# A two-layer decoder step in split float32: another order of the down projection's chunks, of the norm's products and of the last additions, and of the places of the recurrence

## The chip, the cores and the metric

The kernel runs on one core of a Trainium2 chip. The metric is the time of one execution on the device in microseconds; the runs of a kernel are given by their median.

## The reference

One inference step of a decoder with two layers, an mLSTM layer and a forgetting-attention (FoX) layer, each followed by a SwiGLU FFN. A prompt of 1024 tokens behind 16 meta tokens and 8 requests of 8 tokens each go through the same weights: 1104 tokens of 1024 values, d_ff = 2816.

```python
for l in range(DEPTH):
    if l < N_A_LAYERS:
        a, (C, n, m) = mlstm_mixer(rmsnorm(h, norm_a), C0, n0, m0, lead, w_in_a, ...)
        h = h + a                          # out = (rmsnorm(heads) * sigmoid(og)) @ w_out
    else:
        h = h + fox_mixer(rmsnorm(h, norm_b), shared, attend, w_qo_b, q_norm_b, w_out_b)
    h = h + swiglu(rmsnorm(h, norm_ffn[l]), w_gate_up[l], w_down[l])
    if l == N_A_LAYERS - 1:
        shared = shared_kv(h, norm_kv, w_kvf, b_fg_b, k_norm_b)
y = rmsnorm(h, norm_final)

def swiglu(xn, w_gu, w_d):
    gu = xn @ w_gu
    return (silu(gu[..., :D_FF]) * gu[..., D_FF:]) @ w_d
```

It returns y for both groups, the recurrent states of both, and the new keys, values and log-forget values.

## The kernel before

The activations stand transposed: 128 partitions hold features, columns are tokens. The 1104 tokens are three groups (`TS`: 336, 384 and 384 columns, t = 0, 1, 2). Every float32 operand of a product is split into a high part and a low part (L243 the cast on ScalarE, `h`; L244 the subtraction on VectorE, `l`), and each product is three matmuls: high by high, high by low, low by high (L170 to 172, L1589). A norm needs the sum over the features of the squares: `add_sq` squares each of 8 tiles on ScalarE (`nq`, two buffers) and adds it to `ns` on GpSimd, the last one on VectorE; one matmul with ones (`nps`) adds over the partitions; ScalarE takes the root into `nr`, VectorE the reciprocal.

The FFN of a layer ends with the down projection in `ffn`. Its first group takes two rounds of 11 steps; groups 1 and 2 are computed together in seven rounds of a fast 2 x 2 block product (`rounds`: B11, T2, B21, T3, T4, T1, B22), z = 0 to 6. The 11 chunks of a round are taken as `groups`: a single chunk, then five pairs. A step of a pair has 24 matmuls into four PSUM banks (`dps`, of six), a single chunk 12. Rounds z = 1, 4 and 6 go on adding in the banks of the round before. At the last step of a round the banks are added to the residual (L1255; `goes` says to which halves: 12 additions after z = 1, 4 after the others). Each step also starts the split of weights two steps on (`w_split`), of activations (`h_split`), a load of activations on GpSimd's queue (`h_load`) and one of weights five steps on, on SyncE's (`w_load`). During these rounds the program order on TensorE, VectorE and ScalarE is the order in which the code is written.

Between the matmuls of these rounds run the next norm's steps: `norm_x` is a generator, and `ends(t)` makes it the current one of `steps`, from which each step of the down projection takes one piece, two at z > 4:

```python
for _ in range(2 if t and z > 4 else 1):
    next(steps, None)
```

In layer 0 the next norm is that of keys, values and the attention; for groups 0 and 1 it writes its product (L334, VectorE) to a PSUM tile `npy`, copies it to `xh` (L335, ScalarE) and subtracts that for `xl` (L337, VectorE). The group 2 norm comes after the last round; the value products (`tmps`, `first_values`) of the other groups fill in there, from weights that `early` has loaded and split (`first_weights`, the 256 value columns of w_kvf, L237 and L238; other columns, 272 wide, follow). In layer 1 the next norm is the final one (`final`: `fss` one matmul per tile, L1635 to 1657 the root, `fin` transposes, L1670 the product with root and gain).

In layer 0 `mlp` also multiplies the output gates into the heads (L1217): `heads` loads gate tiles `ogc` on GpSimd's queue (L665) into a place of three buffers with the tag `ny`. The pool of these tiles takes the space that the recurrence's tiles held before. There the state C is updated, read by TensorE (L1121), and in the end written out as out_p_C and out_p_n (L927, L928); `gates`, `tmA`, `den`, `ssqA` and the later `rd` and `fA` (L1189 to 1200, the heads' norm) stand beside it. When a new tile takes a place, its first writer waits for what used the place before. Names in the traces carry the tile's name: `vA` and `Ht` are the residual in layer 0 and 1, `slot`, `fs` and `ws` weights, `hr` raw activations.

## Time and profile before

| | us |
|---|---|
| runs, median (lowest to highest) | 2932.83 (2931.76 to 2937.74) |
| profiled execution, its time | 2933.44 |
| profiled execution, its span | 2931.7 |
| TensorE busy in it | 2831.8 (97%) |
| VectorE busy | 1686.1 (58%) |
| ScalarE busy | 1150.9 (39%) |
| GpSimd busy | 826.8 (28%) |

A busy share is over the whole span; a stretch with its own limit shows only in the rows of that stretch. In these, "x" counts instructions, and the granted clock is that of TensorE, 1.00 being full. In a timeline's row the first number is the start, the second the busy time, and in brackets stands the idle time before it and what ended it.

### The profile page before, as it was taken

Reading aid. Unit: us, or ns where it says so; the run is one execution under the profiler, and the core shown is the slowest. Engines: PE = TensorE matmul, PEld = TensorE weight load, DVE = VectorE, ACT = ScalarE, POOL = GpSimd, SP = SyncE. Lnnn points to the kernel's source line nnn. Section 1 sums busy time; section 2 is a strip of 40 time slices with the busy share of each in tenths; the row PEclk is TensorE's granted clock in tenths of the full one; section 3 lists DMA queues with packets and bytes.
Section 4 is the critical chain, followed back from the end, with each engine's and each line's share of the span. In section 5 each row is a group of like instructions: output and inputs, shape, how many; then the busy total and the mean of one; then the engine's idle time right before and its main releaser. Section 6 shows DMA issues by size and latency. Waiting matters only on the chain.

```text
span 2931.7 us, 53400 instructions
## 1 busy us (share of the span) xinstructions
PE 2831.8 (97%) x20709; PEld 2708.8 (92%) x20709; DVE 1686.1 (58%) x3292; ACT 1150.9 (39%) x2103; POOL 826.8 (28%) x1228
## 2 busy tenths in 40 slices
PE   7999999999999999989999999999999999999998
PEld 7989888999999999989999887777899999999998
DVE  5032565876676555763354442677467676665565
ACT  5222363322222244443344453777432222224343
POOL 2011232332232221224353201454232322322122
PEclk9999999999999999999999999999999999999999
DMA  7153545244444375645453685443324454436574
GB/s 249 48 129 94 146 151 151 96 136 154 155 145 151 114 250 189 223 159 159 138 166 127 218 297 202 144 151 128 120 78 143 143 166 145 142 117 225 190 249 151
DMA packets 382631, 464.43 MB, mean 158 GB/s; under 512 B 38594, under 2 KB 303770, under 8 KB 381354
## 3 DMA queue, kind: packets, MB, share of 16 engines
q1 hardware_dynamic: 341058, 323.68, 34.7%
q0 software_dynamic: 37648, 135.03, 14.1%
q8 instruction: 163, 2.67, 0.4%
q10 hardware_dynamic: 3672, 2.31, 0.3%
q14 instruction: 90, 0.74, 0.1%
HBM read 324.63 MB, written 136.29 MB: 157 GB/s over the span
## 4 chain that ended last, share of the span: by engine, by line
PE 77%; DVE 6%; ACT 3%; issue 2%; DMA 2%; POOL 1%; DVEq 0%; SPq 0%; POOLq 0%; ACTq 0%
PE m L1274 22%; PE dps L1589 15%; PE fps L172 4%; PE fps L171 4%; PE fps L170 4%; PE tmps L171 3%; PE tmps L170 3%; PE tmps L172 3%; PE pops L172 2%; PE pops L171 2%; PE pops L170 2%; PE sp L2341 1%; PE op L2428 1%; DVE s L2345 1%; PE bps L170 1%
## 5 line engine op out<-in xcount | busy, mean ns | idle before, releaser
L244 DVE TENSOR_TENSOR slot<-slot,slot 128x1024 fp32r<-128x1024 f32 (+1 forms) x152 | 191.8, 1264 | 119.6 <-ACT slot L243 119.3
L243 ACT CAST slot<-slot 128x1024 fp32r<-128x1024 f32 (+1 forms) x152 | 152.8, 1007 | 184.6 <-PE dps L1589 78.7
L172 PE MATMUL fps<-x0h,slot 128*128 128x336 f32 x688 | 218.2, 317 | 1.6 <-DVE slot L244 1.6
L170 PE MATMUL fps<-x0h,slot 128*128 128x336 f32 x688 | 218.3, 317 | 0.0
L171 PE MATMUL fps<-x0l,slot 128*128 128x336 f32 x688 | 217.4, 316 | 0.0
L1274 PE MATMUL m<-x2h,slot 128*128 128x384 f32 x704 | 193.7, 336 | 0.0
L1274 PE MATMUL m<-x1h,slot 128*128 128x384 f32 x672 | 184.7, 336 | 0.0
L172 PEld LDWEIGHTS fps<-x0h,slot 128*128 128x128 f32 x688 | 129.1, 188 | 2.1 <-DVE slot L244 2.1
L170 PEld LDWEIGHTS fps<-x0h,slot 128*128 128x128 f32 x688 | 129.3, 188 | 0.6 <-ACT slot L243 0.3
L171 PEld LDWEIGHTS fps<-x0l,slot 128*128 128x128 f32 x688 | 129.5, 188 | 0.3
L1274 PEld LDWEIGHTS m<-x2h,slot 128*128 128x128 f32 x704 | 128.5, 188 | 0.0
L1274 PEld LDWEIGHTS m<-x1h,slot 128*128 128x128 f32 x672 | 122.5, 188 | 0.0
L1589 PE MATMUL dps<-T_1h,slot 128*128 128x384 f32 x448 | 119.2, 340 | 2.4 <-ACT T_1h L243 2.4
L1274 PE MATMUL m<-x2l,slot 128*128 128x384 f32 x352 | 118.5, 337 | 0.0
L1589 PE MATMUL dps<-T_2h,slot 128*128 128x384 f32 x448 | 118.5, 340 | 0.0
L244 DVE TENSOR_TENSOR slot<-Ht,slot 128x1024 fp32r<-128x1024 f32 x59 | 83.7, 1419 | 54.5 <-ACT slot L243 54.5
L244 DVE TENSOR_TENSOR slot<-vA,slot 128x1024 fp32r<-128x1024 f32 x59 | 83.6, 1418 | 54.6 <-ACT slot L243 54.6
L1274 PE MATMUL m<-x1l,slot 128*128 128x384 f32 x336 | 112.8, 336 | 0.0
L316 POOL TENSOR_TENSOR ns<-ns,nq 128x384 f32<-128x384 f32 (+1 forms) x68 | 76.6, 1126 | 126.3 <-ACT nq L314 124.0
L1274 PE MATMUL m<-T_2h,slot 128*128 128x384 f32 x352 | 97.7, 338 | 2.0 <-DVE slot L244 2.0
L2368 ACT ACTIVATE s<-s,nb 128x272 f32<-128x272 f32 (+7 forms) x126 | 98.9, 787 | 0.0
L1274 PE MATMUL m<-T_4h,slot 128*128 128x384 f32 x352 | 97.8, 338 | 0.0
(775 smaller groups left out, 9176.8 us busy)
## 6 DMA issues: line engine op xcount, KB each, us to landing
slot<-in_w_down SPq DMA_DIRECT2D x48, 512.0 KB, 4.3
slot<-in_w_gate_up SPq DMA_DIRECT2D x36, 512.0 KB, 4.2
ws<-in_w_down SPq DMA_DIRECT2D x88, 192.0 KB, 3.0
sD<-ws SPq DMA_DIRECT2D x88, 192.0 KB, 2.2
kp<-in_cache_k SPq DMA_DIRECT2D x32, 512.0 KB, 6.0
vp<-in_cache_v SPq DMA_DIRECT2D x32, 512.0 KB, 5.3
hr<-hB_T POOLq DMA_DIRECT2D x40, 384.0 KB, 5.2
vA<-in_w_gate_up SPq DMA_DIRECT2D x26, 512.0 KB, 3.9
```

What stands on the lines that cost most here:

```text
L170: mm(ps, sh, mh, start=first, stop=False)
L171: mm(ps, sh, ml, start=False, stop=False)
L172: mm(ps, sl, mh, start=False, stop=last)
L243: self.nc.scalar.copy(hi, src)
L244: self.nc.vector.tensor_tensor(out=lo, in0=src, in1=hi.bitcast(F32), op=ALU.subtract)
L316: (nc.vector if x >= late else nc.gpsimd).tensor_tensor(out=s, in0=s, in1=sq, op=ALU.add)
L1274: nc.tensor.matmul(u.ps[b], w[p][:, k], x[q][:, k], start=first and k == i == 0, stop=k == 3 and i == 2, skip_group_check=True)
L1589: nc.tensor.matmul(o, p[:, k, ms], q[:, k], start=fresh and k == x == 0, stop=last and k == nk - 1 and x == 2, skip_group_check=True)
L2341: nc.tensor.matmul(ps[z][:, :n], a[r, qs], b[r, at : at + n], start=(y == 0), stop=(y == 2))
L2345: nc.vector.tensor_tensor_reduce(out=ss[z, u][:, at + o : at + e], in0=ps[z][:, o:e], in1=diag[x][:, z] if y else ncb[:, z, at + o : at + ...
L2368: nc.scalar.activation(ss[z, u], ss[z, u], AF.Exp, bias=nb[:, z : z + 1], accum_out=sm[:, u, z : z + 1])
L2428: mm(po[ds[z], :256], vr[:, j0 + x, ds[z]], th[:, x, z], start=(j0 + x == 0), stop=False)
```

## The change

- `groups` puts the single chunk at the end of each round, behind five pairs.
- `norm_x` for groups 0 and 1 of layer 0 makes products 0 and 1 ahead; each later piece copies one product, subtracts its low, and makes the product two ahead. For group 2 the next pair of products is made ahead of the low.
- Two pieces of a norm per step only at odd steps of z > 4, none at the last step of z = 1, else one.
- At the last step of the down projection the four additions come ahead of all squares; for group 2 the last four sums of squares are added on VectorE.
- `first_weights` loads its raw tiles at two earlier steps (into a weight slot and `fs0`) and splits them at the steps where it had loaded and split them before.
- The state C is given its place ahead of `gates` in the pool of layer 0's recurrence, and in the pool of the FFN the first `ns`, `nq`, `nr` and the third gate tile are given theirs first.

```diff
             if then and i % 3 == 2:
                 then(i // 3)
 
+    def place(self, sp, nm, bufs):
+        if nm in self.first:
+            return self.first.pop(nm)
+        return sp.tile([P, SL], F32, name=self.uid(nm), tag=nm, bufs=bufs)
+
     def add_sq(self, H, t, m, sp, x, late=KT - 1):
 
         nc = self.nc
...
         if x == 0:
-            self.sums[t] = sp.tile([P, SL], F32, name=self.uid("ns"), tag="ns", bufs=2)
+            self.sums[t] = self.place(sp, "ns", 2)
             nc.scalar.activation(self.sums[t][:, :n], H[t][:, m], AF.Square)
             return
-        sq = sp.tile([P, SL], F32, name=self.uid("nq"), tag="nq", bufs=2)[:, :n]
+        sq = self.place(sp, "nq", 2)[:, :n]
         nc.scalar.activation(sq, H[t][:, m], AF.Square)
         s = self.sums[t][:, :n]
         (nc.vector if x >= late else nc.gpsimd).tensor_tensor(out=s, in0=s, in1=sq, op=ALU.add)
...
         xh, xl = self.new_x(t)
-        for k in range(KT if psum else 0):
-            y = pp.tile([P, 512], F32, name=self.uid("npy"), tag="n")[:, :n]
-            nc.vector.tensor_tensor(out=y, in0=H[t][:, k], in1=r, op=ALU.mult)
-            nc.scalar.copy(xh[:, k], y)
-            yield
-            nc.vector.tensor_tensor(out=xl[:, k], in0=y, in1=xh[:, k].bitcast(F32), op=ALU.subtract)
-        for z in range(0 if psum else 4):
-            ks = slice(2 * z, 2 * z + 2)
-            y = H[t][:, ks] if inplace else self.ny(self.uid("ny"))[:, :, :n]
+        if psum:
+
+            ys = {}
+
+            def product(k):
+                if k < KT:
+                    ys[k] = pp.tile([P, 512], F32, name=self.uid("npy"), tag="n")[:, :n]
+                    nc.vector.tensor_tensor(out=ys[k], in0=H[t][:, k], in1=r, op=ALU.mult)
+
+            product(0)
+            product(1)
+            for k in range(KT):
+                yield
+                nc.scalar.copy(xh[:, k], ys[k])
+                nc.vector.tensor_tensor(out=xl[:, k], in0=ys.pop(k), in1=xh[:, k].bitcast(F32), op=ALU.subtract)
+                product(k + 2)
+        def scaled(z):
+            y = H[t][:, 2 * z : 2 * z + 2] if inplace else self.ny(self.uid("ny"))[:, :, :n]
             if g is None:
-                nc.vector.tensor_tensor(out=y, in0=H[t][:, ks], in1=r.unsqueeze(1).broadcast_to([P, 2, n]), op=ALU.mult)
+                nc.vector.tensor_tensor(out=y, in0=H[t][:, 2 * z : 2 * z + 2], in1=r.unsqueeze(1).broadcast_to([P, 2, n]),
+                                        op=ALU.mult)
             else:
                 for k in range(2):
                     nc.vector.scalar_tensor_tensor(
                         out=y[:, k], in0=H[t][:, 2 * z + k], scalar=self.gain[:, g + 2 * z + k : g + 2 * z + k + 1],
                         in1=r, op0=ALU.mult, op1=ALU.mult)
+            return y
+
+        ny = None
+        for z in range(0 if psum else 4):
+            ks = slice(2 * z, 2 * z + 2)
+            y = ny or scaled(z)
             nc.scalar.copy(xh[:, ks, :], y)
+
+            ny = scaled(z + 1) if g is None and z < 3 else None
             yield
...
+
+            self.first = {}
+            if heads:
+                for nm in ("ns", "nq", "nr"):
+                    self.first[nm] = sp.tile([P, SL], F32, name=self.uid(nm), tag=nm, bufs=1 if nm == "nr" else 2)
+                self.first["ny"] = self.ny(self.uid("ogc"))
 
             if cb:
                 self.wmin = 4 * 272
...
                     load(nc.gpsimd, 0)
-                    gate = heads(c.enter_context(self.pool("ghp", bufs=2, space=PSUM)), "gh",
-                                 lambda n: sp.tile([P, 2, SL], F32, name=n, tag="ny", bufs=3)[:, 0])
+                    taken = []
+
+                    def third(n):
+                        taken.append(n)
+                        return (self.first.pop("ny") if len(taken) == 3 else self.ny(n))[:, 0]
+
+                    gate = heads(c.enter_context(self.pool("ghp", bufs=2, space=PSUM)), "gh", third)
                     for x in range(3):
                         unit(0, x, x)
                         for _ in range(2):
...
             with cw if not cb else ExitStack():
-                each = lambda t, m, x: self.add_sq(H, t, m, sp, x)
+                each = lambda t, m, x: self.add_sq(H, t, m, sp, x, KT - 1 if t < 2 else KT - 4)
...
         kp = c3.enter_context(self.pool("kA"))
-        gates = kp.tile([P, NT, 16], F32, name="gates")
         tm = kp.tile([P, NT, 104], F32, name="tmA")
         den = kp.tile([P, NT, HA], F32, name="den")
         ssq = kp.tile([P, NT, HA], F32, name="ssqA")
+        self.C = [kp.tile([P, 4, DV + 1], F32, name=f"C{a}") for a in range(3)]
+        gates = kp.tile([P, NT, 16], F32, name="gates")
         self.fin = (tm, den, ssq)
         for i in range(NT):
...
 
-    C = [kp.tile([P, 4, DV + 1], F32, name=f"C{a}") for a in range(3)]
+    C = self.C
     E = mybir.EngineType
     with ExitStack() as cr, self.pool("recAp", bufs=2, space=PSUM) as pp:
         order = ExitStack()
...
                              for i in range(n)]
-        groups = [(0,)] + [(j, j + 1) for j in range(1, NC, 2)]
+        groups = [(j, j + 1) for j in range(0, NC - 1, 2)] + [(NC - 1,)]
         A = lambda i, k: lambda js: wq[:, js[0] : js[-1] + 1, k, i]
         S = lambda i, k: lambda js: sq[:, js[0] : js[-1] + 1, k, i]
         rounds = [(A(0, 0), "B11"), (S(0, 0), "T2"), (A(0, 1), "B21"), (S(1, 0), "T3"), (A(1, 1), "T4"), (S(1, 1), "T1"),
...
                 w_load(i + 5)
+                if len(seq) - 6 < i < len(seq) - 3 and after:
+
+                    early(i - len(seq) + 5, (self.slots[1], fs0)[i - len(seq) + 5])
                 for m in range(4):
                     if fresh:
                         acc[m] = bank("dps")
...
                             pend.append(lambda s=s, m=4 * y + m: square(s, m))
-                        if i == len(seq) - 1:
+                        if i == len(seq) - 1 and m == 3:
                             while pend:
                                 pend.pop(0)()
                 if last and (t, z) in ((0, 1), (1, 4)):
                     pend.append(lambda t=t: ends(t))
                 if len(seq) - 4 < i < len(seq) - 1 and after:
-                    early(i - len(seq) + 3)
+                    early(i - len(seq) + 3, False)
                 for y, k in home.get(i, ()):
                     nc.gpsimd.dma_start(H[y][:, k : k + 2], self.hD[:, k : k + 2, TS[y][0] : TS[y][1]])
-                for _ in range(2 if t and z > 4 else 1):
+
+                for _ in range(2 if t and z > 4 and i % 2 else 0 if t and z == 1 and last else 1):
                     next(steps, None)
                 if not last:
                     for _ in range(2):
...
 @_add(Net)
-def first_weights(self, z):
-
-    if z == 0:
-        self.vhalves = []
-    self.vhalves.append(self.load_w([self.I["w_kvf"][z * 512 : (z + 1) * 512, D : D + 256]], G_KV + 4 * z, nk=4))
+def first_weights(self, z, raw):
+
+    nc = self.nc
+    cut = lambda t: t[:, : 4 * 256].rearrange("p (k n) -> p k n", k=4)
+    if raw is not False:
+        if z == 0:
+            self.vhalves, self.vraw = [], []
+        self.vraw.append(cut(raw))
+        nc.sync.dma_start(self.vraw[z], self.I["w_kvf"][z * 512 : (z + 1) * 512, D : D + 256].rearrange(
+            "(k p) n -> p k n", p=P))
+        return
+    hi, lo = (cut(self.slots[y + self.slot % 4]) for y in (2, 6))
+    self.slot += 1
+    for k in range(4):
+        gk = self.gain[:, G_KV + 4 * z + k : G_KV + 4 * z + k + 1]
+        nc.scalar.activation(hi[:, k], self.vraw[z][:, k], AF.Copy, scale=gk)
+        nc.vector.scalar_tensor_tensor(out=lo[:, k], in0=self.vraw[z][:, k], scalar=gk, in1=hi[:, k].bitcast(F32),
+                                       op0=ALU.mult, op1=ALU.subtract)
+    self.vhalves.append((hi, lo))
```

**VectorE, layer 0, end of round z = 5 and beginning of z = 6.** `npy` is the product, `x1l` the low of the norm of group 1 (L334 and L337 before, L344 and L351 after), L244 are the splits of weights and activations. Before:

```order
L337 TENSOR_TENSOR x1l_11619<-npy_11663,x1h_11618 128x384
L334 TENSOR_TENSOR npy_11686<-vA_99,nr_11582 128x384
L337 TENSOR_TENSOR x1l_11619<-npy_11686,x1h_11618 128x384
L334 TENSOR_TENSOR npy_11690<-vA_99,nr_11582 128x384
L244 TENSOR_TENSOR slot_4731<-slot_4725,slot_4727 128x1024
L244 TENSOR_TENSOR T_1l<-hr_50_11589,T_1h 128x768
L337 TENSOR_TENSOR x1l_11619<-npy_11690,x1h_11618 128x384
L334 TENSOR_TENSOR npy_11727<-vA_99,nr_11582 128x384
L337 TENSOR_TENSOR x1l_11619<-npy_11727,x1h_11618 128x384
```

and now:

```order
L351 TENSOR_TENSOR x1l_11654<-npy_11657,x1h_11653 128x384
L344 TENSOR_TENSOR npy_11696<-vA_99,nr_11594 128x384
L244 TENSOR_TENSOR slot_4735<-slot_4729,slot_4731 128x1024
L244 TENSOR_TENSOR T_1l<-hr_50_11601,T_1h 128x768
L351 TENSOR_TENSOR x1l_11654<-npy_11661,x1h_11653 128x384
L344 TENSOR_TENSOR npy_11734<-vA_99,nr_11594 128x384
L351 TENSOR_TENSOR x1l_11654<-npy_11696,x1h_11653 128x384
L344 TENSOR_TENSOR npy_11738<-vA_99,nr_11594 128x384
L244 TENSOR_TENSOR slot_4736<-fs_5706,slot_4732 128x1024
```

Before, each low stands directly ahead of the next product and both norm pieces stand in every step; now a low is followed by a product of two numbers on, and the pieces come one and two by turns.

**VectorE, layer 1, the end of the last round.** L1255 (now L1290) are the additions of the four banks, L316 (L321) the sums of squares, L1635 (L1674) begins the final root. Before:

```order
L244 TENSOR_TENSOR slot_23024<-slot_23025,slot_23020 128x1024
L244 TENSOR_TENSOR T_4l<-hr_52_29876,T_4h 128x768
L1255 TENSOR_TENSOR Ht_23007<-Ht_23007,dps_29633 128x384
L1255 TENSOR_TENSOR Ht_23007<-Ht_23007,dps_29637 128x384
L1255 TENSOR_TENSOR Ht_23007<-Ht_23007,dps_29641 128x384
L1255 TENSOR_TENSOR Ht_23007<-Ht_23007,dps_29645 128x384
L316 TENSOR_TENSOR ns_29891<-ns_29891,nq_30047 128x384
L1635 MEMSET fr_30050 128x3
```

and now:

```order
L244 TENSOR_TENSOR slot_23024<-slot_23025,slot_23020 128x512
L244 TENSOR_TENSOR T_4l<-hr_52_29876,T_4h 128x384
L1290 TENSOR_TENSOR Ht_23007<-Ht_23007,dps_29633 128x384
L1290 TENSOR_TENSOR Ht_23007<-Ht_23007,dps_29640 128x384
L1290 TENSOR_TENSOR Ht_23007<-Ht_23007,dps_29647 128x384
L1290 TENSOR_TENSOR Ht_23007<-Ht_23007,dps_29654 128x384
L321 TENSOR_TENSOR ns_29903<-ns_29903,nq_30038 128x384
L321 TENSOR_TENSOR ns_29903<-ns_29903,nq_30041 128x384
L321 TENSOR_TENSOR ns_29903<-ns_29903,nq_30044 128x384
L321 TENSOR_TENSOR ns_29903<-ns_29903,nq_30047 128x384
L1674 MEMSET fr_30050 128x3
```

The last step is now the single chunk (512 and 384 wide), and three sums that GpSimd made stand on VectorE, all behind the fourth addition.

**VectorE, layer 0, the last splits and the end of the last round.** L238 and L1756 split value weights. Before:

```order
L337 TENSOR_TENSOR x1l_11619<-npy_11769,x1h_11618 128x384
L244 TENSOR_TENSOR slot_4733<-slot_4724,slot_4729 128x1024
L244 TENSOR_TENSOR T_4l<-hr_52_11670,T_4h 128x768
L238 SCALAR_TENSOR_TENSOR slot_4730<-slot_4724,gain,slot_4726 128x256 x4
L238 SCALAR_TENSOR_TENSOR slot_4731<-slot_4725,gain,slot_4727 128x256 x4
L1255 TENSOR_TENSOR vA_100<-vA_100,dps_11458 128x384
L1255 TENSOR_TENSOR vA_100<-vA_100,dps_11462 128x384
L1255 TENSOR_TENSOR vA_100<-vA_100,dps_11466 128x384
L1255 TENSOR_TENSOR vA_100<-vA_100,dps_11470 128x384
```

and now:

```order
L244 TENSOR_TENSOR T_4l<-hr_52_11667,T_4h 128x384
L1756 SCALAR_TENSOR_TENSOR slot_4734<-slot_4729,gain,slot_4730 128x256 x4
L351 TENSOR_TENSOR x1l_11654<-npy_11738,x1h_11653 128x384
L344 TENSOR_TENSOR npy_11817<-vA_99,nr_11594 128x384
L351 TENSOR_TENSOR x1l_11654<-npy_11777,x1h_11653 128x384
L1756 SCALAR_TENSOR_TENSOR slot_4735<-fs_5706,gain,slot_4731 128x256 x4
L351 TENSOR_TENSOR x1l_11654<-npy_11817,x1h_11653 128x384
L238 SCALAR_TENSOR_TENSOR slot_4736<-slot_4728,gain,slot_4732 128x272
L1290 TENSOR_TENSOR vA_100<-vA_100,dps_11458 128x384
```

The 256-wide value weights are split between pieces of the norm ahead of the last additions; before, all eight stood between the last down split and the additions. GpSimd's three gate loads (L665, L700) keep their rows in its queue; what changes for them is what their places held.

More of the change, by code (lines that the diff above doesn't have):

```diff
@@ L324, in norm_x @@
         nc.tensor.matmul(ps[:, :n], self.ones, self.sums[t][:, :n], start=True, stop=True)
-        r = sp.tile([P, SL], F32, name=self.uid("nr"), tag="nr")[:, :n]
+        r = self.place(sp, "nr", 1)[:, :n]
         nc.scalar.activation(r, ps[:, :n], AF.Sqrt, scale=1.0 / D, bias=self.eps)
```

## The prediction

> **What bounds the kernel now.** I read the page first, then the stretches of the two layers, then what TensorE waits for in them. The profiled execution took 2933.44 us, 0.61 above the median 2932.83; the sum below is made against 2933.44 and the median is taken to follow it. A measurement of this kernel tells about 0.2% (5.9 us) from no change.
>
> ```profile
> span 2931.7 us, 53400 instructions
> PE 2831.8 (97%) x20709; PEld 2708.8 (92%) x20709; DVE 1686.1 (58%) x3292; ACT 1150.9 (39%) x2103; POOL 826.8 (28%) x1228
> ```
>
> TensorE is busy for 2831.8 of 2931.7 us and the change leaves its instructions as many as they are. So only 100 us of idleness, and the stretches at half clock, can be won, and the question is how much of both lies where the change works. In the rows below the columns are the stretch, its length, the busy time of PE, PEld, DVE, ACT, POOL, and then the granted clock, the DMA share and GB/s.
>
> ```profile
> 454.12:458.06 3.94, 3.94 (x27) 3.66 (x25) 3.18 (x6) 1.15 (x3) 1.29 (x3) 1.00 0.95 240
> 458.10:462.90 4.80, 1.45 (x6) 1.05 (x7) 2.73 (x5) 1.08 (x3) 0.00 (x0) 0.75 0.43 139
> 462.90:468.70 5.80, 5.80 (x27) 5.79 (x26) 4.34 (x7) 3.31 (x5) 2.47 (x4) 0.62 0.37 103
> 1179.00:1191.30 12.30, 9.65 (x44) 8.69 (x42) 10.73 (x19) 2.94 (x5) 0.54 (x1) 0.86 0.37 130
> 1180.69:1184.10 3.41, 1.19 (x6) 0.55 (x5) 3.41 (x8) 0.00 (x0) 0.54 (x1) 1.00 0.69 210
> 1184.10:1187.51 3.41, 3.41 (x11) 3.41 (x12) 3.41 (x8) 0.00 (x0) 0.00 (x0) 0.50 0.16 65
> 1187.51:1190.80 3.29, 3.29 (x19) 2.96 (x17) 1.84 (x3) 2.12 (x3) 0.00 (x0) 1.00 0.00 0
> 1277.00:1302.00 25.00, 18.74 (x99) 16.97 (x98) 17.16 (x25) 10.34 (x18) 4.07 (x5) 1.00 0.31 98
> 1310.60:1318.10 7.50, 2.80 (x25) 2.57 (x23) 5.24 (x13) 5.57 (x14) 4.72 (x5) 0.94 0.48 150
> 1318.10:1324.10 6.00, 6.00 (x24) 5.39 (x25) 4.88 (x9) 2.33 (x6) 2.22 (x5) 0.50 0.89 268
> 2765.00:2895.00 130.00, 128.89 (x750) 128.00 (x749) 85.11 (x107) 58.24 (x77) 26.84 (x41) 1.00 0.70 236
> 2920.10:2931.70 11.60, 4.63 (x30) 3.62 (x27) 5.29 (x10) 1.37 (x5) 1.22 (x2) 0.71 0.35 136
> ```
>
> Four stalls of layer 0 lie in code that the change touches: the gates around 458.1 to 462.9, the step from round z = 1 to z = 2 around 1179 to 1191.3, the last two rounds at 1277 to 1302, and the end of the down projection at 1310.6 to 1324.1. Two of them are followed, and one has within it, a stretch at clock 0.50 to 0.62. In layer 1 the rounds stand still for 1.11 of 130.00 us, so little is to be had there. The waits of TensorE in 1051 to 1330 (total us, times, longest), and one of ScalarE there:
>
> ```profile
> PE nps L324 <- DVE ns L316: 4.7, 1, 4.7
> PE dps L1589 <- DVE vA L1255: 2.8, 3, 1.6
> PE dps L1589 <- DVE T_1l L244: 2.6, 2, 1.7
> PE dps L1589 <- ACT T_1h L243: 2.4, 2, 1.2
> ACT x1h L335 <- DVE npy L334: 18.7, 8, 4.2
> ```
>
> **The gates of layer 0 (the order of the places).** The next rows are GpSimd's loads of the gate tiles, and what VectorE does before it can use them.
>
> ```profile
> 448.92 0.23 DVE L1079 COPY den<-nps 128x2 f32<-128x2 f32 x2 [0.19 <-PE nps L1121]
> 453.79 0.55 POOL L665 DMA_DIRECT2D ogc<-ogD  x1 [11.19 <-DVE fA L1193]
> 456.16 1.07 POOL L665 DMA_DIRECT2D ogc<-ogD  x2 [1.82 <-DMA out_p_n<-C]
> 455.50 3.50 DVE L1200 TENSOR_TENSOR vA<-vA,fA 128x1024 f32<-128x1024 f32 x3
> 460.13 0.62 DVE L1217 SCALAR_TENSOR_TENSOR ogc<-ghps,gain,ogc 128x384 f32<-128x384 f32 x1 [1.14 <-DMA ogc<-ogD]
> 461.68 0.62 DVE L1217 SCALAR_TENSOR_TENSOR ogc<-ghps,gain,ogc 128x384 f32<-128x384 f32 x1 [0.93 <-DMA ogc<-ogD]
> ```
>
> The first load goes out at 453.79 because its place held what L1193 reads, the others at 456.16 because theirs held the state that is being written out. They land some 6.3 and 4.5 us after their issue, and VectorE waits 1.14 and 0.93 us for them. With the state's places taken ahead of the gate values, the first load waits for the last product that reads the state, which ends about 448.9, so all three go out by about 450. They then land by 456.4 even at the slower of the two rates, and what is late next is VectorE itself: L1200 ends at 455.50 + 3.50 = 459.0. The products that start at 462.9 would start near 460.9, 2.0 us earlier. The 27 matmuls after the stall take 5.80 us at clock 0.62 and 3.94 at 1.00 (the rows above), so up to 1.86 more is won if the clock stays up; about 1.6 us of idleness stay (458.06 to 459.65), near the 2.2 that cost clock at 1180.69, at the edge of what leaves it up, and I count a quarter of it. **−2.5**, ends 0 (a load that stays late) and −3.9. The waits for the written-out state move to the root tile and the second square tile, first used at about 462 and 516 us, when these writes have long landed: nothing.
>
> **Rounds z = 1 to 2 (no norm step at the last step of z = 1, products two ahead, single chunk last).** In 1179.00 to 1191.30 TensorE stands still for 12.30 − 9.65 = 2.65 us, and 11 matmuls in 1184.10 to 1187.51 take the time in which 19.7 go at full clock (19 in 3.29 us): 1.5 us, and 1.7 with the last of them. The product and its low no longer stand between the twelve additions and the next split. Against it: with the single chunk last, the four sums come 0.53 us apart and not 1.05, so the additions have 1.6 us less before the next round wants the banks; at z = 0 to 1 this leaves the reciprocals in the way, and I take 0.5 us as a new stall. 2.65 + 1.7 − 0.5: **−3.85**, ends −1.5 and −4.4.
>
> **Rounds z = 5 and 6 (products two ahead, two norm steps only at odd steps).** One step of a pair is 24 matmuls, at 3.29 us for 19 (the row at 1187.51) 4.2 us. This is the chain that two norm steps make out of it now:
>
> ```profile
> 1283.95 1.05 ACT L243 CAST slot<-slot 128x1024 fp32r<-128x1024 f32 x1
> 1284.90 0.83 ACT L243 CAST T_2h<-hr 128x768 fp32r<-128x768 f32 x1
> 1285.03 1.23 DVE L244 TENSOR_TENSOR slot<-slot,slot 128x1024 fp32r<-128x1024 f32 x1 [1.49 <-ACT slot L243]
> 1286.17 0.95 DVE L244 TENSOR_TENSOR T_2l<-hr,T_2h 128x768 fp32r<-128x768 f32 x1
> 1287.04 0.55 DVE L337 TENSOR_TENSOR x1l<-npy,x1h 128x384 fp32r<-128x384 f32 x1
> 1287.51 0.56 DVE L334 TENSOR_TENSOR npy<-vA,nr 128x384 f32<-128x384 f32 x1
> 1288.10 0.48 ACT L335 CAST x1h<-npy 128x384 fp32r<-128x384 f32 x1 [2.37 <-DVE npy L334]
> ```
>
> The copy waits for the product, the product stands behind the low, the low behind the split, and the next cast behind the copy: 1.05 + 1.23 + 0.95 + two times (0.55 + 0.56 + 0.48) = 6.4 us, and some 7 with the 0.06 to 0.5 us between engines, for a step of 4.2. Two ahead, the copy finds its product made, so ScalarE has 1.05 + 0.83 + 0.48 (twice at odd steps 0.96) = 2.4 to 2.8 us a step and VectorE 1.23 + 0.95 + 1.11 or 2.22 = 3.3 to 4.4, side by side. The 25.00 − 18.74 = 6.26 us of idleness in 1277 to 1302 go, apart from one step: at the end of the round in which the root falls, the four additions stand behind root, reciprocals and splits: by the order's rows and the durations above the first starts some 7.7 us after nps, and the next round wants its bank after 6.85. **−5.4**, ends −2.7 (VectorE as full as in the first rival) and −6.3.
>
> **The end of layer 0 (early weights, additions ahead of squares, four last sums on VectorE).** Before:
>
> ```profile
> 1309.01 1.71 ACT L237 ACTIVATE slot<-slot,gain 128x256 fp32r<-128x256 f32 x4 [4.19 <-DMA slot<-in_w_kvf]
> 1309.56 3.28 DVE L238 SCALAR_TENSOR_TENSOR slot<-slot,gain,slot 128x256 fp32r<-128x256 f32 x8 [3.35 <-PE dps L1589]
> 1314.07 3.36 POOL L316 TENSOR_TENSOR ns<-ns,nq 128x384 f32<-128x384 f32 x3 [2.63 <-ACT nq L314]
> 1317.45 0.56 DVE L316 TENSOR_TENSOR ns<-ns,nq 128x384 f32<-128x384 f32 x1 [0.89 <-POOL ns L316]
> ```
>
> The last product ends at 1310.6; the additions wait behind eight L238 until 1312.8, the sums on GpSimd take 3.36 us, and nps starts at 1318.07, 7.5 after the product. The value products that fill in last until 1313.4; the rest is the 4.70 us of the row. Afterwards the 256-wide weights are split a step earlier, while the products run, and the additions come at once; of the rest, seven 272-wide L237 (0.43 each by the row, 3.0 us) stand ahead of the last squares on ScalarE, then two squares, one more L237, two squares, and the last sum on VectorE: about 4.75 us after the product. The gap becomes 4.75 − 2.78 = 2.0: −2.7. The stretch after it is 6.00 us at clock 0.50; half of that, 3.0, comes back only if 2.0 us of idleness fall on both sides of a boundary of the clock's windows, and I count a quarter: **−3.5**, ends −0.5 (the 272-wide weights land late and hold up the squares) and −5.7.
>
> **Layer 1.** The same order ends the kernel, without products to fill in.
>
> ```profile
> 2920.04 0.55 DVE L1255 TENSOR_TENSOR Ht<-Ht,dps 128x384 f32<-128x384 f32 x1 [0.50 <-PE dps L1589]
> 2921.43 0.56 DVE L316 TENSOR_TENSOR ns<-ns,nq 128x384 f32<-128x384 f32 x1 [0.83 <-POOL ns L316]
> ```
>
> Now the sum is complete 2.0 us after the last product (2921.43 + 0.56 against 2920.0). Afterwards four sums on VectorE stand behind the fourth addition: 0.65 + four of 0.5, with the third square waiting for the first sum to free its buffer, 2.7 to 2.85 us: +0.7 on the end itself. With the single chunk last, the additions of z = 0 and z = 5 stand behind the four `fin` multiplications: +0.95 for both, from the same 1.6 us, less 0.4 for a stall of that kind that goes. **+1.3**, ends 0 and +4 (five more round ends at 0.55 each).
>
> The split of `first_weights` moves two loads on SP a step or two forward, past loads of the down weights that are asked for five steps ahead, and adds nothing that runs longer; the six sums that go from GpSimd to VectorE are those of the two ends, counted above: 0.
>
> **Sum.** −2.5 − 3.85 − 5.4 − 3.5 + 1.3 = −13.95, 2933.44 − 13.95 = 2919.5 us.
>
> **The clock.** In 1180.69 to 1184.10 TensorE was busy for 1.19 of 3.41 us, no gap in it was longer than 2.2, and the next 3.41 us ran at 0.50, alone between two stretches at 1.00: the clock is set anew in windows of that length. That is why shortened stalls get only a quarter of the clock back. The Trainium skill ("TensorE: Matmul & The Clock Gate", sections "What's actually happening" and "Why this matters for your kernels") says that the clock falls after an idle window of about 3.4 us and asks for no gaps over about 3. By that rule all stalls left here would be too short to cost clock; the trace disagrees where it can be seen, and the rule is the second rival.
>
> **Rivals.**
> First, VectorE is full in the last rounds. One row of layer 1 shows how POOL's sums stretch it:
>
> ```profile
> 2899.13 3.64 POOL L316 TENSOR_TENSOR ns<-ns,nq 128x384 f32<-128x384 f32 x2 [1.14 <-ACT nq L314]
> 2899.87 2.04 DVE L244 TENSOR_TENSOR slot<-slot,slot 128x1024 fp32r<-128x1024 f32 x1
> ```
>
> The split takes 2.04 there and 1.23 at 1285.03. Splits, additions, products and lows of z = 5 and 6 are some 44 us of the 46 that these two rounds take (11 steps of 4.2); three stretched splits fill the rest. Then the last rounds give half (+2.7) and the lows of the weights reach into the tail (+1.8): 2924. Chance 0.18.
> Second, the clock stays up after every shortened stall: 1.4 more at the gates and 2.2 at the tail, 2916. For it speaks that 1.6 us sits at the edge; against it the row 1184.10. Chance 0.14.
> Third, slower: the single chunk at the end of a round leaves the additions 2.1 us where a pair leaves 4.2. If they come late at all twelve round ends of both layers by 1.65 us, the 19.8 us outweigh 13.95 plus 5.9; from about 1.2 us the gain is gone. Against it: the additions are prompt where nothing is ahead of them (0.50 us between at 2920.04), and two of six banks are free at every round end. At 1.65: 2939. Chance 0.03.
> Fourth, the change does little: the loads stay late because of a wait that the order hides, and the 272-wide weights hold the tail, leaving −3.85, −2.7 and +1.3: 2928, within 0.2%. Chance 0.08.
>
> **How the numbers follow.** 0.57 goes to the forecast (own range 2916.5 to 2923), 0.18, 0.14, 0.03 and 0.08 to the rivals. Both ends of the range leave out a tenth: the first and half of the fourth rival lie inside, the second mostly: 2912 to 2928. Faster by over 0.2% means under 2927.0, and holds all but the third and most of the fourth: 0.88; within: 0.09; slower: 0.03.
>
> **What would show it.** Right: the first gate load at about 449 to 450 and L1217 at 459.0; no idleness over 1 us in the rounds z = 1 to 2, 5 and 6; copies of the norm without a wait for their product; a gap of about 2 us ahead of the last nps of layer 0; the last fss about 0.7 us later behind the last product. Wrong: gaps of 0.5 to 1.6 us at the starts of rounds with the wait on the additions, splits of over 1.5 us in z = 5 and 6, or L237 that waits for its weights at the tail.

## The result and the profile after

| | before | changed |
|---|---|---|
| median of 5 runs each, us (lowest to highest) | 2933.34 (2931.76 to 2937.74) | 2918.68 (2914.81 to 2921.81) |
| ratio of the changed kernel to before, 95% interval | | 0.9945 (0.9933 to 0.9956) |
| span of the profiled execution, us | 2931.7 | 2917.0 |

The changed kernel is 14.7 us faster, the forecast was 13.95 for the profiled execution. (The median before stands on two runs more than in the section on the time before, hence 2933.34 and not 2932.83.) The page after, span and busy times:

```profile
span 2917.0 us, 53401 instructions
PE 2823.9 (97%) x20709; PEld 2704.5 (93%) x20709; DVE 1691.4 (58%) x3298; ACT 1152.1 (39%) x2103; POOL 826.1 (28%) x1222
```

TensorE issues the same 20709 matmuls and is busy 7.9 us less. Most of this is half-clock time that is gone: TensorE was busy at half clock for 56.7 us before and for 43.3 us now, and half of the difference is 6.7 us. Not all of it lies in stages that the change touches. The other 6.8 of the 14.7 us of span are idleness. The stretches that answer to those of before (same columns: stretch, length, busy PE, PEld, DVE, ACT, POOL, then clock, DMA share, GB/s):

```profile
451.80:462.80 11.00, 9.83 (x62) 9.32 (x62) 8.11 (x17) 6.04 (x23) 1.51 (x3) 0.94 0.88 130
475.90:490.90 15.00, 13.23 (x83) 12.87 (x83) 7.54 (x13) 4.53 (x8) 4.10 (x6) 1.00 0.60 180
1179.00:1191.30 12.30, 12.30 (x72) 12.30 (x71) 11.24 (x20) 7.60 (x11) 1.02 (x3) 1.00 0.40 130
1251.50:1299.90 48.40, 47.66 (x270) 47.08 (x269) 39.45 (x59) 27.54 (x50) 12.52 (x15) 1.00 0.58 195
1299.90:1303.80 3.90, 2.84 (x24) 2.60 (x23) 3.90 (x9) 2.48 (x6) 2.16 (x4) 1.00 0.46 164
1303.80:1309.80 6.00, 6.00 (x49) 5.74 (x48) 5.93 (x10) 1.61 (x4) 1.56 (x3) 1.00 1.02 299
2903.60:2917.00 13.40, 6.10 (x29) 5.13 (x28) 6.83 (x13) 1.84 (x6) 0.00 (x0) 0.64 0.31 118
```

Around the step from z = 1 to 2 (1179 to 1191.3) TensorE no longer stands still, rounds z = 5 and 6 (1251.5 to 1299.9) hold 0.74 us of idleness, the end of layer 0 (1299.9 to 1303.8) 1.06 and not 4.70, and the 6.00 us behind it hold 49 matmuls at clock 1.00 where before they held 24 at 0.50. The end of the kernel (from 2903.6) is 13.4 us and not 11.7. The waits of TensorE in 1040 to 1330, the wait of ScalarE for products in 1255 to 1312, and two waits of TensorE in layer 1 (total, times, longest):

```profile
PE dps L1627 <- DVE vA L1290: 1.1, 2, 0.7
PE nps L329 <- DVE ns L321: 1.1, 1, 1.1
PE dps L1627 <- DVE x1l L244: 0.7, 1, 0.7
ACT x1h L350 <- DVE npy L344: 5.9, 1, 5.9
PE fss L1692 <- DVE fr L1674: 1.8, 1, 1.8
PE dps L1627 <- DVE Ht L1290: 1.3, 2, 0.6
```

Of the eight waits of ScalarE for a product, 18.7 us in all, one is left, the one for the very first product. The waits of `dps` for the additions are two in each layer. Three of these four are new: in layer 0 the one at 1157.99 (0.39 us), and both of layer 1. The fourth, 0.74 us at 1276.20, stood in the kernel before at 1279.78 with 0.61 us; the waits for the twelve additions behind z = 1 (1.61 and 0.60 us) are gone.

For the table below the first matmul of each round and of its successor were read off the traces (for z6 the end of the last product); in layer 0 "to nps" runs from the last down product to the last norm's matmul, in layer 1 "to fss" likewise, "nps to fgps" is the value products' stretch that begins at half clock in the kernel before. Times in us. The gate stage is given in two parts, from the first to the sixth group of 24 `pops` matmuls and from there to the ninth.

| kernel | gates 1 to 6 | gates 6 to 9 | z0 | z1 | z2 | z5 | z6 | to nps | nps to fgps | layer 1: z0 | z5 | to fss |
|---|---|---|---|---|---|---|---|---|---|---|---|---|
| before | 28.40 | 13.04 | 23.88 | 23.32 | 28.59 | 24.73 | 30.81 | 7.48 | 62.89 | 26.53 | 28.40 | 2.13 |
| changed | 24.12 | 15.03 | 24.44 | 23.39 | 23.32 | 24.86 | 23.55 | 3.85 | 60.10 | 27.40 | 28.38 | 3.20 |
| e1, places alone | 24.09 | 14.90 | 23.88 | 23.32 | 28.59 | 24.72 | 32.05 | 6.28 | 63.22 | 26.55 | 28.44 | 2.13 |
| e2, products alone | 31.78 | 13.05 | 23.88 | 23.32 | 23.32 | 23.96 | 23.47 | 10.49 | 62.88 | 26.55 | 27.51 | 2.12 |
| e3, no places | 29.00 | 13.06 | 24.44 | 23.39 | 23.32 | 24.86 | 23.55 | 3.76 | 60.77 | 27.42 | 28.38 | 3.20 |
| e4, single first | 25.83 | 14.88 | 23.88 | 23.32 | 23.32 | 23.97 | 23.47 | 3.99 | 60.10 | 26.55 | 27.51 | 3.19 |
| e5, late weights | 24.06 | 18.27 | 24.44 | 23.40 | 23.32 | 24.85 | 23.55 | 7.43 | 62.29 | 27.40 | 28.38 | 3.20 |
| e6, sums on GpSimd | 24.12 | 15.02 | 24.44 | 23.40 | 23.32 | 24.85 | 23.56 | 7.23 | 61.60 | 27.42 | 28.38 | 3.64 |
| e7, two pieces | 24.31 | 17.35 | 24.44 | 23.40 | 23.32 | 26.79 | 24.98 | 3.83 | 60.73 | 27.42 | 29.88 | 3.20 |
| e8, free places | 24.24 | 17.39 | 23.88 | 23.32 | 23.32 | 23.96 | 23.47 | 4.00 | 60.74 | 26.55 | 27.51 | 3.19 |
| e9, lag | 24.03 | 18.55 | 23.88 | 23.32 | 23.32 | 23.96 | 23.47 | 4.31 | 60.72 | 26.53 | 27.48 | 1.95 |
| e10, as e4 | 25.46 | 13.04 | 23.88 | 23.32 | 23.32 | 23.97 | 23.47 | 4.01 | 60.72 | 26.55 | 27.51 | 3.19 |
| e11, as e9, no places | 29.11 | 13.04 | 23.88 | 23.32 | 23.32 | 23.96 | 23.47 | 4.15 | 60.78 | 26.55 | 27.51 | 1.95 |

With the chunks in one order, a round with no stall repeats to 0.03 us from kernel to kernel, so single profiled executions tell these terms apart. The whole span doesn't: the first `pops` matmul falls at 446.7 to 453.2 us in the thirteen profiled executions, a scatter of 6.5 us that hasn't to do with the rounds.

### The profile page after: what moved, and what is told of

It reads as the page before. It is cut to its first block, busy times and chain, and to the rows that moved or that the text cites. A ratio compares the mean times of both kernels' runs of the same rounds, so it can differ in the third digit from the quotient of the medians.

```text
span 2917.0 us, 53401 instructions
## 1 busy us (share of the span) xinstructions
PE 2823.9 (97%) x20709; PEld 2704.5 (93%) x20709; DVE 1691.4 (58%) x3298; ACT 1152.1 (39%) x2103; POOL 826.1 (28%) x1222
## 4 chain that ended last, share of the span: by engine, by line
PE 78%; DVE 6%; ACT 2%; DMA 2%; issue 2%; POOL 1%; DVEq 0%; SPq 0%; ACTq 0%; POOLq 0%
PE m L1309 22%; PE dps L1627 15%; PE fps L172 4%; PE fps L171 4%; PE fps L170 4%; PE tmps L170 3%; PE tmps L171 3%; PE tmps L172 3%; PE pops L172 2%; PE sp L2394 2%; PE pops L170 2%; PE pops L171 2%; DVE s L2398 1%; PE op L2481 1%; PE mmA L170 1%
## 5 line engine op out<-in xcount | busy, mean ns | idle before, releaser
L244 DVE TENSOR_TENSOR slot<-slot,slot 128x1024 fp32r<-128x1024 f32 (+1 forms) x152 | 193.8, 1276 | 140.2 <-ACT slot L243 140.0
L244 DVE TENSOR_TENSOR slot<-Ht,slot 128x1024 fp32r<-128x1024 f32 x59 | 83.7, 1419 | 54.5 <-ACT slot L243 54.5
L244 DVE TENSOR_TENSOR slot<-vA,slot 128x1024 fp32r<-128x1024 f32 x59 | 83.7, 1418 | 54.6 <-ACT slot L243 54.6
L321 POOL TENSOR_TENSOR ns<-ns,nq 128x384 f32<-128x384 f32 (+1 forms) x62 | 75.9, 1224 | 103.0 <-ACT nq L319 101.1
```

Of the source, the lines that this page charges most:

```text
L244: self.nc.vector.tensor_tensor(out=lo, in0=src, in1=hi.bitcast(F32), op=ALU.subtract)
L321: (nc.vector if x >= late else nc.gpsimd).tensor_tensor(out=s, in0=s, in1=sq, op=ALU.add)
```

## Experiments

**Places alone (e1), and everything but the places (e3).** In e1 the kernel before gets the new order of places:

```diff
-        gates = kp.tile([P, NT, 16], F32, name="gates")
         tm = kp.tile([P, NT, 104], F32, name="tmA")
         ...
+        self.C = [kp.tile([P, 4, DV + 1], F32, name=f"C{a}") for a in range(3)]
+        gates = kp.tile([P, NT, 16], F32, name="gates")
```

with `self.first` and `place` as in the change; in e3 the changed kernel goes back to the old order.

> The kernel before with the new places alone. Theory (the places pay as forecast, and what the profile of the changed kernel shows ahead of 454 us is chance): the products after the gates start 2 us earlier against the matmul before them, the clock stays up, part of it is lost again where a weight tile of w_out_a is late; 1 to 3 us faster in all, about 2931. Rival (the places cost something in the recurrence, the 2.8 us by which the changed kernel is later at 453 us): the stretch up to 434 us is 1 to 3 us longer here too, and the time is that of before within 1 us.

> The changed kernel with the old places. Theory: 1 to 3 us slower than the changed kernel, the stretch at half clock at 460 comes back. Rival (places cost as much as they give): the same within 1 us, and the stretch up to 434 us is 1 to 3 us shorter than in the changed kernel.

Measured: e1 2934.55 (median of 11) against 2932.66, ratio 1.0004 (0.9995 to 1.0013): no gain, where the theory had 1 to 3 us. e3 2918.84, ratio to before 0.9951 (0.9937 to 0.9964), the same as the changed kernel, as its rival had it, though the half clock at 460 did come back (6.83 us from 460.42). Yet inside the stage the places do what they were forecast to do. In the changed kernel the three loads go out together, behind VectorE's copy of the last product that reads the state, and VectorE takes both gates at once behind L1235; further on a new stall appears:

```profile
451.70 1.61 POOL L700 DMA_DIRECT2D ogc<-ogD  x3 [6.83 <-DVE den L1114]
461.15 1.14 DVE L1252 SCALAR_TENSOR_TENSOR ogc<-ghps,gain,ogc 128x384 f32<-128x384 f32 x2
481.94 0.55 PE L1251 MATMUL ghps<-ident,vA 128*128 128x128 f32 x3 [1.76 <-DVE ogc L1252]
ACT slot L243 <- DMA slot<-in_w_out_a: 6.0, 2, 5.5
```

The gate that TensorE waits for at 481.94 stands on VectorE behind the split of a weight tile of w_out_a, and that split waits for the tile's DMA. In e9 the same place reads:

```profile
PE ghps L1251 <- DVE ogc L1252: 3.7, 1, 3.7
ACT slot L243 <- DMA slot<-in_w_out_a: 8.0, 2, 7.7
```

In the nine profiled executions with the new places gates 1 to 6 take 24.0 to 25.8 us; in the four with the old ones (before, e2, e3, e11) 28.4 to 31.8. Gates 6 to 9 take 13.04 to 13.06 in the four, and 13.04 (e10) to 18.55 in the nine. So about 5 us are won ahead and 0 to 5.5 given back behind; the net over both parts is 40.5 on the mean of nine against 42.6 of four. Counted from the start of the execution even this is gone: the first group begins at 449.9 us on the mean of the nine and at 448.3 of the four, the ninth at 490.5 (485.7 to 492.6) and at 490.9 (490.6 to 491.5). That fits the timed runs of e1 and e3, which show no gain. What makes the first 450 us scatter, and whether the places have a share in it, stays open, and so does why e10, with the new places, met no late tile.

**Products two ahead and the numbers of pieces alone (e2), and two pieces in the changed kernel (e7).** e2 is the kernel before with the `psum` branch of the change's `norm_x` and its line

```diff
-                for _ in range(2 if t and z > 4 else 1):
+                for _ in range(2 if t and z > 4 and i % 2 else 0 if t and z == 1 and last else 1):
```

and e7 is the changed kernel with this line as before.

> The kernel before with the products two ahead and the new numbers of norm pieces per step alone. Theory (the ping-pong of product and copy is the cause of the stalls in rounds z = 2 and 6 of layer 0): round z = 2 goes from 28.6 to under 24 us and z = 6 from 30.8 to under 25.5, 9 to 12 us faster, about 2922. Rival (the single chunk's place is what makes room): z = 2 or z = 6 keeps over half of its excess, and the gain stays under 6 us.

> The changed kernel with two norm pieces at every step of z > 4 and one at the last step of z = 1, as before. Theory (the products ahead alone take the stalls away; the numbers of pieces matter little): z = 2 and z = 6 of layer 0 within 0.5 us of 23.3 and 23.5, the time the same. Rival (two pieces at every step fill VectorE in the last rounds, and the piece behind z = 1 delays the twelve additions): z = 6 over 1 us longer, or z = 2 over 1 us longer.

Measured: e2 2923.03 (median of 6), ratio 0.9969 (0.9957 to 0.9981). Round z = 2 loses 5.27 us, z = 5 0.77, z = 6 7.34, and z = 5 of layer 1 0.89: 14.3 together. Then 3.0 are given back at once, since the end of layer 0 gets longer (7.48 to 10.49): the rounds are done before the value weights have come. ScalarE, VectorE and TensorE there, in e2:

```profile
1294.00 1.71 ACT L237 ACTIVATE slot<-slot,gain 128x256 fp32r<-128x256 f32 x4 [6.92 <-DMA slot<-in_w_kvf]
1301.58 6.22 DVE L238 SCALAR_TENSOR_TENSOR slot<-slot,gain,slot 128x272 fp32r<-128x272 f32 x8
PE nps L324 <- DVE ns L316: 7.7, 1, 7.7
```

The wait for the weights' DMA is 6.92 us and was 4.19; the last sum then stands behind eight L238. So the products ahead and the pace of the pieces together take the stalls of the rounds away, wherever the single chunk stands, and the end of layer 0 is where a faster round goes if the weights aren't earlier too. e7 tells the two apart.

e7: 2922.14 (median of 4), 0.9955 (0.9939 to 0.9970). z = 2 stays at 23.32, as the theory said, but z = 5 takes 1.93 us more than in the changed kernel, z = 6 1.43 (its rival was right there) and z = 5 of layer 1 1.50. Its waits of `dps` for the additions in layer 0 and 1:

```profile
PE dps L1627 <- DVE vA L1290: 3.1, 2, 2.7
PE dps L1627 <- DVE Ht L1290: 1.9, 2, 1.3
```

Pieces at every step stand ahead of the four additions at the end of z = 5, and these ahead of the next round. The longest wait, 2.7 us at 1278.44, is followed by 3.41 us at half clock from 1278.21, and z = 6 itself has no wait: its 1.43 us are the clock's. So, as far as e2 and e7 tell together, the ping-pong of product and copy was the cause at z = 2, where the products ahead are enough, and of 5.83 of the 7.34 us at z = 6 (30.81 to 24.98); the pace of the pieces matters at the end of z = 5.

**The single chunk first again (e4, repeated as e10).**

```diff
-        groups = [(j, j + 1) for j in range(0, NC - 1, 2)] + [(NC - 1,)]
+        groups = [(0,)] + [(j, j + 1) for j in range(1, NC, 2)]
```

> The changed kernel with the single chunk first in each round, as before. Theory (the place of the single chunk costs 0.6 us at z = 0 of layer 0 and 0.9 at z = 0 of layer 1, and gives nothing that the products ahead don't give): these two rounds fall back to 23.9 and 26.5 us, the rest stays, about 1.4 us faster than the changed kernel. Rival (the single chunk at the end makes room for the norm's pieces and brings the end nearer): z = 2 or z = 6 of layer 0 is over 1 us longer, or the ends are, and the time is 1 us or more longer.

> The changed kernel with the single chunk first once more, on the same chip as the two others of this call, for the comparison; all rounds as in its first run (z = 0 of layer 0 23.88, z = 6 23.47), 2909 to 2914.

Measured: e4 2912.61, ratio 0.9933 (0.9920 to 0.9947); e10 2912.15, 0.9931 (0.9917 to 0.9945). The waits of `dps` for additions are gone; of TensorE's waits in the down projections and norms of both layers these are left in e4 (besides those of `fss` for the root and one of 0.3 us of `fin`):

```profile
PE nps L329 <- DVE ns L321: 1.2, 1, 1.2
PE fss L1692 <- DVE fr L1674: 1.8, 1, 1.8
```

z = 0 and 5 of layer 0 fall by 0.56 and 0.89 us, z = 1 and 6 by 0.07 each, z = 0 and 5 of layer 1 by 0.85 and 0.87: 3.3 us that the single chunk at the end of the round costs in the changed kernel. It gives nothing in return that is above 0.2 us: z = 2 and z = 6 are as short, and the end of layer 0 is 3.99 against 3.85. The theory had 1.4; it had missed z = 5, where the changed kernel takes as long as the kernel before (24.86 and 24.73 us). The rounds show these 3.3 us; the timed runs alone don't, since the intervals of e4 and e10 overlap that of the changed kernel (0.9933 to 0.9956).

**The 256-wide weights late (e5), and the last sums on GpSimd (e6).** e5 is the changed kernel with the old `first_weights` and without the early call:

```diff
-                if len(seq) - 6 < i < len(seq) - 3 and after:
-                    early(i - len(seq) + 5, (self.slots[1], fs0)[i - len(seq) + 5])
...
-                    early(i - len(seq) + 3, False)
+                    early(i - len(seq) + 3)
```

and e6 with the old places of squares and sums:

```diff
-                each = lambda t, m, x: self.add_sq(H, t, m, sp, x, KT - 1 if t < 2 else KT - 4)
+                each = lambda t, m, x: self.add_sq(H, t, m, sp, x)
...
-                        if i == len(seq) - 1 and m == 3:
+                        if i == len(seq) - 1:
```

> The changed kernel with the 256-wide value weights loaded and split as before, behind the last steps. Theory (they are what held the end of layer 0): from the last down product of layer 0 to nps it takes 9 to 11 us and not 3.85, the half clock behind it comes back (2.8 us), 6 to 10 us slower than the changed kernel, about 2926. Rival (the additions ahead of the squares and the sums on VectorE made the end short): nps stays within 6 us, under 3 us slower.

> The changed kernel with three of the last four sums on GpSimd and each square behind its own addition, as before, in both layers. Theory (behind a single chunk GpSimd's 1.1 us per sum are the longer way): fss in layer 1 comes 3.3 to 3.7 us after the last product and not 3.2, nps of layer 0 within 4 to 5; the time the same or up to 2 us longer. Rival (the sums on VectorE behind the fourth addition are what made the end later): fss at about 2.1 as before, 1 us faster.

Measured: e5 2923.19, 0.9959 (0.9946 to 0.9972); e6 2924.98, 0.9967 (0.9955 to 0.9979). Both ends of layer 0 go back to 7.4 and 7.2 us. First e5, then e6:

```profile
1295.05 1.71 ACT L237 ACTIVATE slot<-slot,gain 128x256 fp32r<-128x256 f32 x4 [7.31 <-DMA slot<-in_w_kvf]
PE nps L329 <- DVE ns L321: 4.6, 1, 4.6
```

```profile
1298.85 6.20 DVE L238 SCALAR_TENSOR_TENSOR slot<-slot,gain,slot 128x272 fp32r<-128x272 f32 x7
1304.97 0.54 DVE L321 TENSOR_TENSOR ns<-ns,nq 128x384 f32<-128x384 f32 x1
PE nps L329 <- DVE ns L321: 4.4, 1, 4.4
PE fss L1692 <- DVE fr L1674: 2.2, 1, 2.2
```

Neither edit makes the short end alone. With late weights everything behind them is late; with the sums on GpSimd the one sum that is left on VectorE stands behind seven L238, where in the changed kernel the four sums stand between them:

```profile
1300.35 0.56 DVE L321 TENSOR_TENSOR ns<-ns,nq 128x384 f32<-128x384 f32 x1
1300.82 0.50 DVE L238 SCALAR_TENSOR_TENSOR slot<-slot,gain,slot 128x272 fp32r<-128x272 f32 x1
1301.24 0.55 DVE L321 TENSOR_TENSOR ns<-ns,nq 128x384 f32<-128x384 f32 x1
```

Both theories had the direction; e5 was 4.5 us slower than the changed kernel's median (6 to 10 expected, its `nps` at 7.43 and not 9 to 11; in its profiled execution the end and the stretch behind it cost 5.8 us more), and e6 missed altogether in layer 0, where 4 to 5 was expected and 7.23 came. In layer 1, which has no weights to split there, GpSimd's sums cost only 0.44 us (3.64 against 3.20).

**Free places for the last squares (e8), and squares one addition behind (e9).** Both with the single chunk first. e8 takes the third and fourth square of group 2 out of the two buffers of `nq`:

```diff
+        if t == 2 and x >= KT - 2:
+            if x == KT - 2:
+                self.sq2 = self.ny(self.uid("sq"))
+            sq = self.sq2[:, x - KT + 2, :n]
```

and e9 lets each square follow the next bank's addition:

```diff
-                        if i == len(seq) - 1 and m == 3:
-                            while pend:
+                        if i == len(seq) - 1:
+                            while len(pend) > (m < 3):
```

> The changed kernel with the single chunk first and with two more places for the last squares (in a free place of raw activations), so that no square waits for a sum. Theory (the third and fourth square of the end wait for the sums to free their buffers): fss in layer 1 comes 0.4 to 0.6 us earlier behind the last product than with the single chunk first alone (3.19), nps of layer 0 up to 0.4; 2912. Rival (the squares are not what the sums wait for): the same ends within 0.1 us.

> The changed kernel with the single chunk first, and at the last step each square and its sum one addition behind its own addition in place of all behind the fourth. Theory (four sums that depend on one another, 0.62 us each, stand behind the fourth addition and are the end's length; a pair's additions are 1.05 us apart and leave VectorE room for three of them): fss in layer 1 comes 1.8 to 2.2 us behind the last product and not 3.19, nps of layer 0 at most 3.4 and not 3.99; 1 to 2 us faster than the single chunk first alone. Rival (sums between the additions push these back, as the ping-pong did): fss at 3 us or later, no gain.

> The kernel with the single chunk first and the squares one addition behind, with the old places. Theory (the places save 2.5 us and more up to the products behind the gates, and lose some 1.7 of them to a weight tile that comes late): 13.5 us or more from the first to the third part of these products and not 11.03, no late tile behind them; 1 to 3 us slower than with the new places. Rival (the whole kernel shows nothing of it, as in the first two comparisons): the same within 1 us.

Measured: e8 2908.89, 0.9908 (0.9895 to 0.9922), with rounds and ends as in e4 to 0.03 us, `fss` at 3.19: its rival was right. Its median is lower all the same; no stage of its profiled execution (2913.67 us) shows where that could come from, and it stays unexplained. e9 2913.34, 0.9935 (0.9921 to 0.9949), `fss` at 1.95 and not 3.19, as its theory had it, but `nps` of layer 0 at 4.31, 0.3 later, where 3.4 at most was expected, and no gain in the whole. The last squares and sums in layer 1, in e4 first, where the third square waits for a sum, then the sums in e8 and in e9:

```profile
2897.93 1.19 ACT L319 ACTIVATE nq<-Ht 128x384 f32<-128x384 f32 x2 [1.99 <-DVE ns L321]
2897.35 2.54 DVE L321 TENSOR_TENSOR ns<-ns,nq 128x384 f32<-128x384 f32 x4
```

```profile
2899.31 1.21 DVE L326 TENSOR_TENSOR ns<-ns,nq 128x384 f32<-128x384 f32 x2
2900.62 1.22 DVE L326 TENSOR_TENSOR ns<-ns,sq 128x384 f32<-128x384 f32 x2
```

```profile
2904.34 0.55 DVE L321 TENSOR_TENSOR ns<-ns,nq 128x384 f32<-128x384 f32 x1
2905.07 0.56 DVE L321 TENSOR_TENSOR ns<-ns,nq 128x384 f32<-128x384 f32 x1 [0.18 <-ACT nq L319]
PE fss L1692 <- DVE fr L1674: 0.5, 1, 0.5
```

In e8 no square is waited for, and four sums into one tile still take 2.5 us, 0.62 each. Where another instruction stands behind a sum, as at 1300.35 in the rows of the changed kernel, it starts 0.47 us after it. In e9 two of the four are made between the additions. That is worth 1.2 us at the end of the kernel, and the timed runs (2913.34 against 2912.15 of e10 on the same chip) don't show it; the gate stage of its profiled execution lost 3.74 us to the late weight tile. e11, the same with the old places, 2914.30, 0.9934 (0.9920 to 0.9948): gates 29.11 and 13.04 us, and 13.87 us from the first to the third part and not 11.03, as its theory had it; the whole is the same within 1 us, as its rival said.

## Why the prediction came out

The sum, 2919.5, was 0.8 above the median. Its terms were not that good: in the profiled execution they come to −18.0 us where the forecast has −13.95, and 3.2 us outside the terms (2.2 ahead of the gates, 1.0 in the down projection's first round, where weights came late in the same order as before) make up most of the difference. That the sum fell so near is luck; that the change is worth 13 to 20 us, the interval of the timed runs, is not.

- Gates, −2.5: −2.3 in this execution (39.15 against 41.44 us over both parts), −2.1 on the mean of all, counted from the first group. Counted from the start of the execution the ninth group begins at 490.77 us and began at 490.81, and e1 and e3 show no gain in the whole, so the term can't be called right. The 2 us and the whole of the clock came, together 4.3 up to the sixth group, and 2.0 went again. The step that failed is "what is late next is VectorE itself": what was late next behind the gates was a w_out_a tile, and the range of 0 to −3.9 was meant for the gate loads, not for it.
- z = 1 to 2, −3.85: −5.27 + 0.56 + 0.08 = −4.6. The new stall at z = 0 was sized right (0.5 against 0.56). The loss was read too small, as in the next term: 42 matmuls start in the stretch of 1179 to 1191.3, which take 7.4 us at the pace of a round with no stall (132 in 23.32 us), so 4.9 of its 12.30 us were lost and not 4.35.
- z = 5 and 6, −5.4: −7.1. The term that was mis-sized is the loss before: TensorE's idleness in 1277 to 1302, 6.26 us, is not all of it. 97 matmuls start there, which take 17.1 us at the pace of a round with no stall, so 7.9 of the 25.00 us were lost; around each gap the profile counts as busy what is slower than that pace. The stall behind the root was sized right: 0.85 against 0.89 by e4.
- End of layer 0, −3.5: −3.6 to nps and −2.8 behind it (62.89 to 60.10), −6.4. The step that failed is the clock: a gap of 2.0 us was forecast at one in four to leave it up; the gap was 1.06 us, and the clock stayed. That the early weights and the sums on VectorE are both needed is what e5 and e6 add.
- Layer 1, +1.3: +0.6 in all rounds and 1.8 at the end, +2.4. `fss` was put at 2.7 to 2.85 us behind the last product and came at 3.2; the cause given (the third square waits for a buffer) is wrong, as e8 shows: with buffers for all, four sums into one tile take the same 2.5 us. And the three `fss` and the transposes behind them ran partly at half clock (0.64 over 2903.6 to 2917.0; the stretch before had 0.71).

Of the rivals, the second, a clock that stays up behind the shortened stalls, came true at the gates and at the end of layer 0, but, as far as the counts of the last section tell, by the phase and size of the gaps and not by a rule of 3 us. VectorE full in z = 5 and 6 did not come with the change's pace, but e7 shows where it begins: with two pieces at every step the two rounds lose 3.4 us, 1.4 of them to the clock. The slower case, a price at each of twelve round ends, was real at four of them, two in each layer, at 0.56 to 0.9 us, and under 0.1 at the others, far from the 1.65 that it needed. Two signs of being wrong did show without making it wrong: waits for the additions of 0.39 to 0.74 us at the starts of four rounds, and at the end of layer 0 one wait of 0.45 us of L237 for its weights.

## What to carry to other kernels

Read a stall's successor before pricing its removal: here the gates' 5 us met a weight tile that had been in time in all four executions with the old places, and e2 paid 3 of its 14 us at the next stage at once. Where rounds repeat to 0.03 us, compare rounds and ends, not spans: beside a gain of 15 us there was a cost of 3.3 inside the change, which the total hid, and with that edit taken back the median is 2912 us (0.9931 to 0.9933 of before). An edit that only works with another (early weights and sums between their splits) loses its gain when either is taken away, so undo edits one at a time from the changed kernel and don't only add them to the old one.

## What the runs showed of the clock

The clock's half-speed stretches are multiples of 3.41 us (but for one that the end of the kernel cuts), and in each execution they start on one raster of windows of this length, which lies otherwise in every execution. For each window at full clock the idleness of TensorE in it was added up, over all thirteen traces. With 1.87 us and more, 69 of 69 were followed by one at half clock; with 1.1 to 1.87 us 46 of 160; with 0.9 to 1.1 none of 84. Below 0.9 us it was 7 of some 10500, with 0.37 to 0.76 us idle; these lie at 184 to 186 and at 1793 to 1812 us and hold matmuls of 8 or 32 columns, so the idleness in the profile isn't the whole of what the clock goes by. The Trainium skill ("TensorE: Matmul & The Clock Gate", section "What's actually happening") says that the clock falls after an idle window of about 3.4 us, and that the window is free-running. These traces agree with the second. The first they show too lax, and the measurement decides: just over half of a window idle was always enough, and a third of it sometimes. The same two gaps, 1.2 and 1.67 us, in the last rounds of the kernel before and of e1 show what the raster does; first before, then e1, each window with the one behind it:

```profile
1300.20:1303.60 3.40, 1.86 (x10) 1.86 (x11) 2.85 (x5) 0.94 (x2) 0.00 (x0) 1.00 0.00 0
1303.60:1307.00 3.40, 3.37 (x19) 3.06 (x19) 2.22 (x3) 1.22 (x2) 0.00 (x0) 1.00 0.13 25
```

```profile
1301.20:1304.60 3.40, 1.73 (x9) 1.55 (x9) 2.85 (x5) 0.62 (x2) 0.00 (x0) 0.97 0.00 0
1304.60:1308.00 3.40, 3.40 (x12) 3.40 (x12) 2.54 (x3) 1.53 (x2) 0.00 (x0) 0.53 0.03 7
```

With 1.54 us idle the next stretch ran 19 matmuls, with 1.67 us 12, and z = 6 of e1 took 32.05 us and not 30.81. The whole didn't pay for it: the norm behind it came 6.28 us after the last product and not 7.48, since what held it there were the splits of the value weights, whose DMA came as late as before (ScalarE waited 4.22 us for it and 4.19 before). So in this kernel a window with 1.1 to 1.9 us of stall costs up to 1.7 us more (half of one window at half clock), by chance, and bringing it below 1.1 us can be worth more than the stall's length.
